# A convolution with max pooling: other steps with five products, column maxima by one reduction, another order

## The chip, the cores and the metric

The kernel runs on one core of one Trainium2 chip. The time is the device time of one execution in microseconds; where several runs were made, their median is given. The engines that matter are PE (TensorE, matrix products), DVE (VectorE), ACT (ScalarE), POOL (GpSimd) and SP (SyncE, here only for issuing transfers).

## The reference

A 3x3 convolution of 16 images, 64 input and 128 output channels, 64x64 pixels, with padding of one, and then the maximum of each 2x2 block:

```python
batch, c_in, h, w, c_out, k = 16, 64, 64, 64, 128, 3
x_pad = np.pad(x, ((0, 0), (0, 0), (1, 1), (1, 1)))
conv[b, co] += weight[co, ci, kh, kw] * x_pad[b, ci, kh:kh+h, kw:kw+w]
...
output[b, c, i, j] = np.max(conv[b, c, 2*i:2*i+2, 2*j:2*j+2])
```

Input and output are float32; the products are made of bfloat16 values and summed in float32.

## The kernel before

**Tiles.** Two images lie together on the 128 partitions, 64 input channels each. There are 8 such pairs, and each is cut into 4 quarters of 16 image rows: 32 *steps*, numbered 0 to 31 (steps 2 and 3 stand for quarters 3 and 2 of pair 0). A step yields 8 pooled rows of 64 columns, 512 numbers per output channel, for each of its two *halves* (half 0 and half 1 are the two images). 512 float32 are one bank of the accumulation memory; there are eight banks, the tiles `acc_84` to `acc_91` in the listings below. The halves' matmuls use the two row halves of the array and run side by side, as two lanes.

**Products.** For a pooled row four input rows d0 to d3 are needed. Instead of 2 x 3 tap rows on them, sums of rows and sums of weights are used. A *product* is three matmuls (the three column taps) of 512 or 504 columns for one half. There are two kinds of step.

- *Four products (W).* P2 with weights GM on d1-d2 (row sum E) and P0 with G0 on d2-d0 (part of row sum D) go into a first bank; P3 with G2 on d3-d1 (rest of D) and P1 with GP on d1+d2 (row sum S) into a second, which begins as a copy of the first after P2. That copy is the *seed* (SE, on ACT). The first bank is read out negated (EV, on ACT) to on-chip memory.
- *Five products (K).* PA1, PA2 with D2 on d2 and G0 on d0 go into the first bank, PB1, PB2 with D0 on d1 and G2 on d3 into the second, straight from the loaded rows; PR with G1 on d1+d2 (row sum KS) comes last, into the second. No seed, and one row sum in place of three.

In both kinds the maximum of the two pooled rows is taken before the last product, which is common to both rows: the row maximum (MX, on DVE, L376) puts max(second bank, EV) back in the second bank, then P1 or PR is added there. After it ACT copies the odd columns out (OD, L382), and DVE takes the maximum of the even columns in the bank and that copy (the column maximum, CM, L396) into the output tile `o` of the step, from which SP stores (ST, L416). The first bank is free after EV, the second after CM, and the next product that begins a bank takes the one that has been free longest.

**Row sums.** E, S (512 elements per partition) and D (1024) of each W step are made by POOL where `ON_GPSIMD` names them (L89, POOL), otherwise by DVE (L88, DVE); KS by DVE always. A sum on POOL waits for the last sum that DVE has before it in the order.

**Start.** Weights come in by one transfer, are cast (g0, g1, g2) and summed (D2, D0, GS, GM, GP), turned on PE against an identity (T..., L149) and copied out to `wt` (V..., L164 on ACT, L166 and L168 on DVE). Eight matmuls of ones (L524) run ahead of that. Input of pair 0 comes in seven pieces, the other pairs in two or three each (LX, issued on POOL's queue, L105), turning float32 to bfloat16 on the way. Steps 0 and 2 begin with their products cut into two half products of four pooled rows (F and H), step 1 partly (G).

**End.** The last step, 31, is worked in two parts of four pooled rows, each part's second sum in banks of its own (four banks for two halves): SL is its seeds (four copies of 256, L367), Z its P3, ML its row maxima (L372), Q its P1, ODh and CMh its odd copies and column maxima (L402, L410), U its stores (L425): before, U.0 stores part 0 of both images, U.1 and U.2 part 1 of one image each, U.1 on ACT's queue.

**Order.** The string `ORDER` lists all steps of the work by name (MX.8.1 is the row maximum of step 8, half 1), and every engine runs its own instructions in that order. A product of one half is held back until the other lane has one to go with it. Instructions wait for their data and for buffers through semaphores; an engine that waits holds all that is queued behind. Pools: 12 output tiles `o`, 14 of D, 12 each of E and S, 3 of KS, 8 each of `ev` and `od`.

## Time and profile before

| | |
|---|---|
| median of 3 runs | 101.95 us (101.53 to 102.34) |
| the profiled execution | 101.44 us, its span 99.7 us |
| granted TensorE clock, mean | 0.99 |
| matmul records | 913 |
| column maxima on DVE, step 0 to 30 | 62, mean 417 ns |
| read-outs EV on ACT | 52 negated, mean 617 ns; 12 copied, 595 ns |
| seeds on ACT | 48 of 512, mean 595 ns; 4 of 256 for the last step |
| DMA | 17.23 MB, mean 173 GB/s |

In the profile an engine's line gives its busy time, share of the span and instructions. The strips cut the span into 40 slices of 2.5 us and show the busy share of each in tenths. A group's row has the code line, engine, operation, output and input tiles with partitions x elements and type, the count, then busy time and mean ns of one, then the engine's idle time just before them with what ended it. A timeline row has the start, the length, and the instructions that ran on from one another under one line (`x2`), and in brackets an idle time before it with its releaser. Instructions of one engine overlap a little, so the distance of two starts is less than the duration of the first. Seen durations of matmuls are longer than their distance for the same reason. In the rows on transfers the last number is the time from issue to landing.

### The profile page before, as it was taken

To read this page: it belongs to the slowest core of one execution; us is meant where nothing else is said; L and a number is where in the kernel's file an instruction comes from. 1 tells how busy PE (TensorE), PEld (TensorE's weight loads), DVE (VectorE), ACT (ScalarE), POOL (GpSimd) and SP (SyncE) were. 2 spreads that over 40 slices of the span, in tenths; PEclk is the share of its full clock that TensorE was granted. 3 is DMA by queue.
4 is the path that set the end of the run, shared out by engine and by line. 5 is a ranking of instruction groups with operands and counts; after the bars stand their busy time and mean duration, and the time that the engine had idled before them with its cause. 6 is when DMAs were issued, how large, how long until landed. Compare 5 with 4: busy or idle time off the path is not lost.

```text
span 99.7 us, 2526 instructions
## 1 busy us (share of the span) xinstructions
PE 94.1 (94%) x913; PEld 60.8 (61%) x913; DVE 86.2 (86%) x192; ACT 83.2 (83%) x192; POOL 72.8 (73%) x74
## 2 busy tenths in 40 slices
PE   6999999999999999999999999999999999998830
PEld 2588864455755545566687666556578768863410
DVE  3568899999999999999999999889896899888660
ACT  5453967899898589979999988999999999999730
POOL 5996689647846992696196993994979996999300
PEclk9999999999999999999999999999999999999995
DMA  2999999999999999986709999955330285063462
GB/s 57 167 170 157 184 203 208 205 221 207 227 230 230 263 276 197 183 229 77 144 3 285 147 205 227 357 187 180 105 105 7 68 268 193 0 217 105 138 202 81
DMA packets 12316, 17.23 MB, mean 173 GB/s; under 512 B 912, under 2 KB 10256, under 8 KB 12304
## 3 DMA queue, kind: packets, MB, share of 16 engines
q0 software_dynamic: 3168, 8.39, 47.6%
q1 hardware_dynamic: 8992, 8.62, 26.6%
q8 instruction: 7, 0.11, 0.5%
q10 hardware_dynamic: 144, 0.07, 0.2%
q14 instruction: 5, 0.04, 0.1%
HBM read 17.07 MB, written 8.39 MB: 255 GB/s over the span
## 4 chain that ended last, share of the span: by engine, by line
PE 83%; ACT 9%; DVE 3%; issue 1%; DVEq 0%; ACTq 0%
PE acc L182 78%; ACT ev L342 4%; PE acc L524 4%; ACT acc L356 3%; PE acc L149 2%; ACT od L382 2%; DVE acc L376 1%; DVE acc L372 1%; DVE o L396 0%; DVE o L410 0%; ACT od L402 0%; DVEq L561 0%; DVEq L376 0%; ACTq L356 0%
## 5 line engine op out<-in xcount | busy, mean ns | idle before, releaser
L182 PEld LDWEIGHTS <-wt 64*128 64x128 bf16 x882 | 57.8, 94 | 31.5 <-issue 3.9
L182 PE MATMUL acc<-wd,wt 64*128 64x512 bf16 (+3 forms) x330 | 60.0, 365 | 0.0
L376 DVE TENSOR_TENSOR acc<-acc,ev 128x512 f32<-128x512 f32 x62 | 41.4, 694 | 3.8 <-ACT ev L342 2.0
L182 PE MATMUL acc<-ws,wt 64*128 64x512 bf16 (+3 forms) x162 | 37.4, 369 | 1.0 <-DVE acc L372 0.7
L182 PE MATMUL acc<-we,wt 64*128 64x512 bf16 (+3 forms) x162 | 36.6, 369 | 0.0
L342 ACT ACTIVATE ev<-acc 128x512 f32<-128x512 f32 x52 | 31.0, 617 | 0.6 <-PE acc L182 0.3
L356 ACT COPY acc<-acc 128x512 f32<-128x512 f32 x48 | 28.3, 595 | 3.1 <-DVE o L396 1.6
L396 DVE TENSOR_TENSOR o<-acc,od 128x256 f32<-128x256 f32 x62 | 24.5, 417 | 1.9 <-ACT od L382 1.3
L89 POOL TENSOR_TENSOR ws<-xb 128x512 bf16<-128x512 bf16 x18 | 20.6, 1155 | 6.5 <-PE acc L182 4.5
L89 POOL TENSOR_TENSOR we<-xb 128x512 bf16<-128x512 bf16 x17 | 19.5, 1154 | 7.6 <-DVE wd L88 3.9
L382 ACT COPY od<-acc 128x256 f32<-128x256 f32 x62 | 22.7, 389 | 2.2 <-PE acc L182 1.6
L89 POOL TENSOR_TENSOR wd<-xb 128x1024 bf16<-128x1024 bf16 (+1 forms) x10 | 20.3, 2030 | 5.2 <-DVE we L88 5.2
L182 PE MATMUL acc<-xb,wt 64*128 64x252 bf16 (+7 forms) x192 | 23.9, 319 | 0.0
L105 POOL DMA_DIRECT2D xb<-in_x_dram x22 | 12.2, 567 | 0.8 <-POOLq L547 0.8
L88 DVE TENSOR_TENSOR wd<-xb 128x1024 bf16<-128x1024 bf16 (+1 forms) x17 | 10.8, 667 | 0.0
L340 ACT COPY ev<-acc 128x512 f32<-128x512 f32 x12 | 6.7, 595 | 3.1 <-PE acc L182 3.1
L182 PE MATMUL acc<-ks,wt 64*128 64x504 bf16 (+1 forms) x36 | 7.3, 377 | 0.0
L524 PE MATMUL acc<-const-bfloat16-1.0 128*128 128x512 bf16 x8 | 3.6, 625 | 0.8 <-PEq L547 0.8
L88 DVE TENSOR_TENSOR we<-xb 128x512 bf16<-128x512 bf16 (+1 forms) x10 | 3.7, 391 | 0.0
L88 DVE TENSOR_TENSOR ws<-xb 128x512 bf16<-128x512 bf16 x8 | 3.3, 418 | 0.0
L88 DVE TENSOR_TENSOR ks<-xb 128x512 bf16<-128x512 bf16 x6 | 2.6, 438 | 0.7 <-DMA xb<-in_x_dram 0.7
L524 PEld LDWEIGHTS <-const-bfloat16-1.0 128*128 128x128 bf16 x8 | 1.0, 136 | 2.4 <-issue 2.4
(25 smaller groups left out, 20.2 us busy)
## 6 DMA issues: line engine op xcount, KB each, us to landing
out_dram<-o SPq DMA_DIRECT2D x31, 256.0 KB, 2.7
xb<-in_x_dram POOLq DMA_DIRECT2D x7, 496.0 KB, 10.4
xb<-in_x_dram POOLq DMA_DIRECT2D x6, 528.0 KB, 10.6
xb<-in_x_dram POOLq DMA_DIRECT2D x3, 128.0 KB, 4.5
wraw<-in_weight_dram SPq DMA_DIRECT2D x1, 288.0 KB, 2.8
xb<-in_x_dram POOLq DMA_DIRECT2D x1, 272.0 KB, 6.5
xb<-in_x_dram POOLq DMA_DIRECT2D x1, 256.0 KB, 7.2
xb<-in_x_dram POOLq DMA_DIRECT2D x1, 224.0 KB, 5.2
```

Of the source, the lines that this page charges most:

```text
L88: return on_vector(nc.vector.tensor_tensor(**args))
L89: return on_gpsimd(nc.gpsimd.tensor_tensor(**args))
L105: nc.gpsimd.dma_start(out=xb[p][:, 1 + lo : 1 + hi, :], in_=rows_of(p, lo, hi))
L149: nc.tensor.transpose(tp[:, k * CO : (k + 1) * CO], wq[:, j : j + 2, :].rearrange("a b c -> a (b c)"), ident,)
L182: nc.tensor.matmul(acc[t][:, i0:i1, o0:o1], wt[lo : lo + CI, m0 + kw - h, :], rows(lo, i0, i1, c0, c1), start=start and kw == 1, stop=True ...
L340: nc.scalar.copy(out=ev[s, h], in_=acc[t])
L342: nc.scalar.mul(ev[s, h], acc[t], -1.0)
L356: nc.scalar.copy(out=acc[tb[s, h]], in_=acc[ta[s, h]])
L376: nc.vector.tensor_tensor(out=t, in0=t, in1=ev[s, h], op=MAX)
L382: nc.scalar.copy(out=od[s, h], in_=acc[tb[s, h]][:, :, 1::2])
L396: nc.vector.tensor_tensor(out=ot[s][:, h], in0=acc[t][:, :, 0::2], in1=od[s, h], op=MAX)
L524: nc.tensor.matmul(acc[n].rearrange("p a b -> p (a b)"), ones[:, 0:128], ones, start=True, stop=True, skip_group_check=True)
```

## The change

The kinds of the steps change: five-product steps were 0, 2, 4, 10, 16 and 23, and are 0, 2, 11, 20 and 31. There are 27 four-product steps in place of 26. Since the last step is now of five products, a new function begins its second sums: `last_start` (Y) takes the two banks of a part and puts the D0 product of that part in them; Z then adds G2 on the rows themselves and Q adds G1 on KS. It has no seeds.

Sixteen column maxima (`REDUCED`) are made without ACT's odd copy: one `tensor_reduce` on DVE reads all 512 elements of the bank as pairs and writes 256 (L397 in the changed kernel).

All six turn-outs are on ACT, also that of GM and GP with the factor 0.5 (MP), and all three casts. The weight sum GS goes from POOL to DVE. The list of sums on POOL is another: of the 27 four-product steps POOL makes 17 E, 16 S and 10 D, and for step 1 the first half of E in place of the first half of D.

The order is new throughout. Among others, the loads of pairs 5 to 7 are issued one after the other, and the last step's stores end with part 0 of both halves (U.0). Line numbers shift: row maximum L384, column maximum L404, odd copy L390, read-outs L348 and L350, seed L364, half row maximum L380, odd half copy L410, column half L418, sums L87 on DVE and L88 on POOL, loads L104.

```diff
-    TYPES = "KWKWKWWWWWKWWWWWKWWWWWWKWWWWWWWW"
+    TYPES = "KWKWWWWWWWWKWWWWWWWWKWWWWWWWWWWK"
     ON_GPSIMD = """
-        Da E.3 S.3 E.5 S.5 E.6 E.7 S.9 S.6 E.13 D.11 S.8 S.11 S.13 E.17 E.14 E.15 E.18 E.12 S.12 E.19 S.17 S.18
...
+        Ea E.3 S.3 E.4 S.5 E.6 S.6 E.9 E.8 D.7 E.10 S.8 D.10 S.16 S.13 D.13 S.12 E.16 E.15 E.17 E.25 S.15 E.18
...
-    TURNED_BY_SCALAR = ("D2", "G0", "D0")
-    CAST_BY_SCALAR = ("g0", "g2")
-    REDUCED = ()
+    TURNED_BY_SCALAR = ("D2", "G0", "G2", "G1", "D0", "MP")
+    CAST_BY_SCALAR = ("g0", "g1", "g2")
+    REDUCED = ((10, 1), (13, 1), (14, 0), (14, 1), (20, 1), (18, 0), (18, 1), (21, 0), (22, 0), (23, 0), (23, 1), (24, 0), (26, 1), (27, 1), (27, 0), (30, 1))
...
     def last_product(part):
         span = (0, R // 2) if part == 0 else (R // 2, R)
-        pair_of_taps(tb, (N - 1, part), GP, step1(row["s", N - 1]), False, None, span)
+        block = GP if TYPES[N - 1] == "W" else G1
+        pair_of_taps(tb, (N - 1, part), block, step1(row["s", N - 1]), False, None, span)
+
+    def last_start(part):
+        span = (0, R // 2) if part == 0 else (R // 2, R)
+        take(tb, (N - 1, part), 0)
+        take(tb, (N - 1, part), 1)
+        pair_of_taps(tb, (N - 1, part), D0, k_rows(N - 1, 0), True, None, span)
 
     def last_edges(part):
         span = (0, R // 2) if part == 0 else (R // 2, R)
-        pair_of_taps(tb, (N - 1, part), G2, step2(row["d", N - 1], 1), False, None, span)
+        w = TYPES[N - 1] == "W"
+        rows = step2(row["d", N - 1], 1) if w else k_rows(N - 1, 2)
+        pair_of_taps(tb, (N - 1, part), G2, rows, False, None if w else R - 1, span)
...
-        "GS": lambda: sbuf_sum(False, out=gsum, in0=g0, in1=g2, op=ADD),
+        "GS": lambda: sbuf_sum("GS" not in ON_GPSIMD, out=gsum, in0=g0, in1=g2, op=ADD),
...
-        "SL": seed_last, "Z": last_edges, "ML": rowmax_half, "U": last_store,
+        "SL": seed_last, "Y": last_start, "Z": last_edges, "ML": rowmax_half, "U": last_store,
...
     ORDER = """
-        CM.2.1 CM.2.0 EV.1.0 PA1.4.1 PB1.4.1 G.2.0 MX.1.0 PA2.4.1 EV.1.1 MX.1.1 PR.0.0 LX.3.0 E.3 S.3 LX.3.1 E.5
...
+        P2.9.1 ST.2 ST.3 ST.4 ST.0 OD.6.0 CM.6.0 ST.6 ST.1 SE.9.1 PA1.11.1 P0.9.0 EV.9.0 E.8 D.7 LX.5.0 LX.5.1
+        LX.6.0 LX.6.1 LX.7.0 LX.7.1 S.10 D.12 D.14 E.13 S.7 KS.11 D.17 P2.7.1 P2.7.0 SE.7.0 P0.9.1 PA2.11.1
...
```

Three places of the order. First DVE's queue in the middle, around the column maxima of step 8; `we`, `wd`, `ws` and `ks` are the row sums E, D, S and KS. Before:

```order
L376 TENSOR_TENSOR acc_87<-acc_87,ev 128x512
L376 TENSOR_TENSOR acc_86<-acc_86,ev 128x512
L88 TENSOR_TENSOR we<-xb_102 128x512
L88 TENSOR_TENSOR ks<-xb_101 128x512
L376 TENSOR_TENSOR acc_85<-acc_85,ev 128x512
L376 TENSOR_TENSOR acc_91<-acc_91,ev 128x512
L396 TENSOR_TENSOR o<-acc_87,od 128x256
L396 TENSOR_TENSOR o<-acc_86,od 128x256
L376 TENSOR_TENSOR acc_88<-acc_88,ev 128x512
L376 TENSOR_TENSOR acc_84<-acc_84,ev 128x512
```

The rows are the row maxima of step 8, the sums E of step 20 and KS of step 16, row maxima of steps 16 and 13, the column maxima of step 8, and row maxima of step 11. After the change:

```order
L404 TENSOR_TENSOR o<-acc_84,od 128x256
L404 TENSOR_TENSOR o<-acc_86,od 128x256
L397 TENSOR_REDUCE o<-acc_90 128x256
L384 TENSOR_TENSOR acc_85<-acc_85,ev 128x512
L87 TENSOR_TENSOR we<-xb_101 128x512
L404 TENSOR_TENSOR o<-acc_87,od 128x256
L87 TENSOR_TENSOR wd<-xb_100 128x1024
L87 TENSOR_TENSOR ws<-xb_100 128x512
L384 TENSOR_TENSOR acc_84<-acc_84,ev 128x512
L404 TENSOR_TENSOR o<-acc_85,od 128x256
L384 TENSOR_TENSOR acc_89<-acc_89,ev 128x512
```

These are the column maxima of steps 8 and 11 (half 0), the reduction of step 10, the row maximum of step 8 (half 1), E of step 19, the column maximum of step 10, D of step 15 and S of step 14, the row maximum of step 12, the second column maximum of step 8, and a row maximum of step 12. Step 8's two halves now stand apart, and a reduction and three sums lie between the row maximum of its second half and the column maximum or close ahead of them.

Second, ACT's queue at the end, where `od` is an odd copy and `ev` a read-out. Before:

```order
L367 COPY acc_86<-acc_85 128x256
L367 COPY acc_90<-acc_89 128x256
L367 COPY acc_91<-acc_85 128x256
L367 COPY acc_87<-acc_89 128x256
L382 COPY od<-acc_88 128x256
L382 COPY od<-acc_84 128x256
L342 ACTIVATE ev<-acc_85 128x512
L342 ACTIVATE ev<-acc_89 128x512
L402 COPY od<-acc_87 128x128
L402 COPY od<-acc_91 128x128
L402 COPY od<-acc_86 128x128
L402 COPY od<-acc_90 128x128
```

After the change:

```order
L350 ACTIVATE ev<-acc_87 128x512
L350 ACTIVATE ev<-acc_90 128x512
L348 COPY ev<-acc_89 128x512
L348 COPY ev<-acc_91 128x512
L390 COPY od<-acc_84 128x256
L410 COPY od<-acc_85 128x128
L410 COPY od<-acc_86 128x128
L410 COPY od<-acc_90 128x128
L410 COPY od<-acc_87 128x128
```

The four seed copies are gone; the two read-outs of the last step (now copies, not negated) come ahead of one odd copy and the four half copies.

Third, POOL's queue, where the loads of pairs 5 to 7 are issued (`xb_102` to `xb_104`). Before:

```order
L89 TENSOR_TENSOR ws<-xb_98 128x512
L89 TENSOR_TENSOR we<-xb_98 128x512 x2
L89 TENSOR_TENSOR ws<-xb_99 128x512
L89 TENSOR_TENSOR ws<-xb_98 128x512
L105 DMA xb_102<-in_x_dram 128x2112
L89 TENSOR_TENSOR we<-xb_100 128x512
L89 TENSOR_TENSOR wd<-xb_99 128x1024
L89 TENSOR_TENSOR ws<-xb_99 128x512 x2
L105 DMA xb_102<-in_x_dram 128x1984
```

After the change:

```order
L88 TENSOR_TENSOR ws<-xb_98 128x512
L88 TENSOR_TENSOR we<-xb_99 128x512 x2
L88 TENSOR_TENSOR wd<-xb_98 128x1024
L104 DMA xb_102<-in_x_dram 128x2112
L104 DMA xb_102<-in_x_dram 128x1984
L104 DMA xb_103<-in_x_dram 128x2112
L104 DMA xb_103<-in_x_dram 128x1984
L104 DMA xb_104<-in_x_dram 128x2112
L104 DMA xb_104<-in_x_dram 128x1984
L88 TENSOR_TENSOR we<-xb_99 128x512
L88 TENSOR_TENSOR ws<-xb_99 128x512
L88 TENSOR_TENSOR wd<-xb_99 128x1024
```

Six loads now follow one another behind the sum D of step 7, with no sum between them.

More of the change, by code (lines that the diff above doesn't have):

```diff
@@ L520 @@
+        SE.30.0 OD.29.0 CM.29.0 OD.29.1 ST.20 ST.25 ST.19 CM.29.1 ST.28 ST.29 ST.18 D.30 P0.30.1 P3.30.1
+        PA2.31.0 P0.30.0 EV.30.1 MX.30.1 EV.30.0 P3.30.0 PA2.31.1 MX.30.0 Y.1 EV.31.0 Z.1 ML.1.0 EV.31.1 ML.1.1
+        Y.0 Z.0 ML.0.0 ML.0.1 S.30 P1.30.0 P1.30.1 OD.30.1 OD.30.0 CM.30.1 CM.30.0 ST.30 Q.1 ODh.1.0 Q.0 ODh.1.1
+        ODh.0.1 ODh.0.0 CMh.0.0 CMh.1.1 U.2 CMh.1.0 U.1 CMh.0.1 U.0
     """
```

100 lines of the change are left out of this document (47 added, 53 removed).

## The prediction

> **What bounds the kernel now.** I read the page first: the engines' busy time, the strip of 40 slices, and the chain that ended last.
>
> ```profile
> PE 94.1 (94%) x913; PEld 60.8 (61%) x913; DVE 86.2 (86%) x192; ACT 83.2 (83%) x192; POOL 72.8 (73%) x74
> ...
> PE   6999999999999999999999999999999999998830
> ...
> DVE  3568899999999999999999999889896899888660
> ...
> GB/s 57 167 170 157 184 203 208 205 221 207 227 230 230 263 276 197 183 229 77 144 3 285 147 205 227 357 187 180 105 105 7 68 268 193 0 217 105 138 202 81
> ...
> PE 83%; ACT 9%; DVE 3%; issue 1%; DVEq 0%; ACTq 0%
> ```
>
> PE is full from the fifth microsecond nearly to the end and holds 83% of the chain. DVE, though, is a strip of nines from slice 7 to 25 (15 to 62 us), with small gaps only after that. So PE bounds, and DVE stands right behind it through the middle.
>
> Next the timeline of PE, for its rate and for the end of its unbroken stretch.
>
> ```profile
> 5.77 1.47 PE L182 MATMUL acc<-xb,wt 64*128 64x256 bf16 x24
> ...
> 89.69 0.38 PE L182 MATMUL acc<-ws,wt 64*128 64x512 bf16 x1
> ...
> 89.91 0.38 PE L182 MATMUL acc<-ws,wt 64*128 64x504 bf16 x1
> ...
> 90.12 0.38 PE L182 MATMUL acc<-ws,wt 64*128 64x504 bf16 x1
> ...
> 90.99 0.38 PE L182 MATMUL acc<-ws,wt 64*128 64x512 bf16 x1
> 91.70 0.81 PE L182 MATMUL acc<-ws,wt 64*128 64x512 bf16 x5 [0.33 <-DVE acc L376]
> 92.21 1.73 PE L182 MATMUL acc<-wd,wt 64*128 64x512 bf16 x18
> ```
>
> One lane starts a matmul at 89.69, 89.91 and 90.12; the other lane's lie between, so four matmuls take 0.43: 0.1075 each. A product of one half-step (six matmuls over a pair of lanes) is 0.645, a half product 0.32. Of the 882 convolution matmuls, 36 start at 90.99 or later, so 846 lie before (by the code 714 full and 132 of half width). At that rate they need 76.8 + 7.1 us, and the last seven turns 0.4: from 5.77 that is 90.1. The row says 90.99, so PE ran at its floor for 85 us and lost 0.9. Behind it come 12 full and 24 half matmuls, 2.6 us: they could end at 93.6.
>
> DVE's own rate, from its timeline in the middle:
>
> ```profile
> 42.47 0.75 DVE L396 TENSOR_TENSOR o<-acc,od 128x256 f32<-128x256 f32 x2
> 43.13 1.29 DVE L376 TENSOR_TENSOR acc<-acc,ev 128x512 f32<-128x512 f32 x2
> 44.33 0.75 DVE L396 TENSOR_TENSOR o<-acc,od 128x256 f32<-128x256 f32 x2
> ...
> 46.40 0.68 DVE L88 TENSOR_TENSOR wd<-xb 128x1024 bf16<-128x1024 bf16 x1
> 47.00 0.42 DVE L88 TENSOR_TENSOR ks<-xb 128x512 bf16<-128x512 bf16 x1
> ...
> 48.53 0.75 DVE L88 TENSOR_TENSOR ws<-xb 128x512 bf16<-128x512 bf16 x2
> 49.20 0.69 DVE L376 TENSOR_TENSOR acc<-acc,ev 128x512 f32<-128x512 f32 x1
> ```
>
> The next start tells what one costs in a queue: row maximum 0.60, column maximum 0.33, long sum (D) 0.60, short sum (S, E, KS) 0.335.
>
> **The change, part by part.** *One product less.* 133 products in place of 134: six matmuls, -0.645, taken as **-0.6** on the path that is full. The last step's extra product in halves is within that count.
>
> *DVE's added load.* Sixteen column maxima read a whole bank instead of half. The trace has no such instruction. Its lower bound is the column maximum, 0.33, which also writes 256 elements; its upper bound is this row of POOL, 1.15:
>
> ```profile
> L382 ACT COPY od<-acc 128x256 f32<-128x256 f32 x62 | 22.7, 389 | 2.2 <-PE acc L182 1.6
> L89 POOL TENSOR_TENSOR ws<-xb 128x512 bf16<-128x512 bf16 x18 | 20.6, 1155 | 6.5 <-PE acc L182 4.5
> ```
>
> I take 0.60, the row maximum's, since that is the DVE row that reads as many elements out of the same memory. So 16 x 0.27 = +4.3 us of DVE work. Four more short sums and one KS less add 1.0, the half D 0.4. The weight turns that leave DVE return 1.8, a weight sum that comes to it costs 0.4. DVE ends with about 4 us more.
>
> The Trainium skill, "VectorE: DVE Perf Modes", section "Rules for kernel authors", speaks against this part: it says of tensor_reduce on a hot path "Expect 1× — it's the slowest DVE op", and to restructure. No row here shows the operation. By the page the cost would stand at the upper part of the bounds rather than the lower.
>
> *Whether DVE then holds PE.* For this I count DVE's lateness: the clock less its own work so far. Before, up to the middle:
>
> ```profile
> L376 DVE TENSOR_TENSOR acc<-acc,ev 128x512 f32<-128x512 f32 x26 | 17.0, 693 | 1.0 <-ACT ev L340 0.5 <-ACT od L382 0.2
> L396 DVE TENSOR_TENSOR o<-acc,od 128x256 f32<-128x256 f32 x23 | 8.7, 416 | 0.0
> L88 DVE TENSOR_TENSOR wd<-xb 128x1024 bf16<-128x1024 bf16 x10 | 6.6, 682 | 0.0
> L88 DVE TENSOR_TENSOR ks<-xb 128x512 bf16<-128x512 bf16 x5 | 2.2, 442 | 0.7 <-DMA xb<-in_x_dram 0.7
> L88 DVE TENSOR_TENSOR ws<-xb 128x512 bf16<-128x512 bf16 x4 | 1.7, 420 | 0.0
> L88 DVE TENSOR_TENSOR we<-xb 128x512 bf16<-128x512 bf16 x4 | 1.6, 418 | 0.0
> ...
> 10.48 1.30 DVE L376 TENSOR_TENSOR acc<-acc,ev 128x512 f32<-128x512 f32 x2 [0.47 <-ACT ev L340]
> ```
>
> These rows are the groups up to 44.6 us, and last DVE's first row maximum on its timeline. 26 x 0.60 + 23 x 0.335 + 10 x 0.60 + 13 x 0.335 + 0.7 for halves = 34.4; the second column maximum of the pair at 44.33 starts at 44.66, lateness 10.3. At the first row maximum it was 10.48 - 1.4 = 9.1. So it grew by 1.2 in 34 us: DVE almost never waited.
>
> In the changed order I take the column maximum of step 8, half 1, whose bank step 14's first product needs. Ahead of and with it DVE has 25 row maxima 15.0, 23 column maxima 7.7, one reduction 0.6, 11 long sums 6.6, 15 short ones 5.0, halves 0.9: 35.7 us. PE's work ahead of that product is 277 full and 132 half matmuls and seven turns: 37.3, so 43.1 from 5.77. DVE's lateness has a floor from step 2's row maximum, which needs 18 half products (5.77 + 5.8 + 0.5 = 12.1) and has 3.7 of DVE work ahead: 8.4. With the growth of before it is 9.6; I take 9.1, a little past the middle: the waits for ACT stay, but ACT has less to do. Then DVE is done at 44.8 and PE starts that product 1.8 late (1.1 to 2.3), where before lost 0.9 in all: **+0.9**. Counted along the order at these rates, a column maximum of before precedes the product that takes its bank by 4 us or more here, in the changed order by 1.7 to 2, and this stays so up to the end. So DVE becomes the bound in the middle, and the late stage has about 1.6 us to give before it costs more.
>
> *The end.* The last steps as they are:
>
> ```profile
> 91.24 1.19 ACT L367 COPY acc<-acc 128x256 f32<-128x256 f32 x4 [0.23 <-PE acc L182]
> ...
> 92.75 0.76 DVE L396 TENSOR_TENSOR o<-acc,od 128x256 f32<-128x256 f32 x2 [0.78 <-ACT od L382]
> 93.75 1.58 DVE L372 TENSOR_TENSOR acc<-acc,ev 128x256 f32<-128x256 f32 x4 [0.24 <-ACT ev L342]
> ...
> 96.21 0.49 DVE L410 TENSOR_TENSOR o<-acc,od 128x128 f32<-128x128 f32 x2 [0.17 <-ACT od L402]
> ```
>
> PE's work could end at 93.6, but the four seed copies (1.19) stand ahead of everything on ACT, DVE's half row maxima start at 93.75, and the last column maximum ends at 96.70: 3.1 behind PE's own work. With a five-product last step the seeds go; its four half row maxima are ready while PE still has step 30's and the last products. What stays behind the last matmul is one odd half copy (0.21) and up to four column halves (0.21 each, from 0.49 for two), with the reduction of step 30 (0.60) partly ahead: 1.5. So **-1.6**. Were the reduction and step 30's column maximum wholly behind, 0.6 of that goes.
>
> The final store is now of both halves:
>
> ```profile
> out_dram<-o SPq DMA_DIRECT2D x1, 128.0 KB, 1.9
> out_dram<-o SPq DMA_DIRECT2D x1, 64.0 KB, 1.7
> ...
> out_dram<-o SPq DMA_DIRECT2D x31, 256.0 KB, 2.7
> ...
> out_dram<-o SPq DMA_DIRECT2D x1, 256.0 KB, 9.8
> ```
>
> The first two rows are the last step's stores: **+0.2**.
>
> *What I cost at nothing.* Three more turn-outs and a cast go to ACT. Its rows:
>
> ```profile
> 4.14 1.70 PE L149 MATMUL acc<-ident,wq 128*128 128x128 bf16 x16
> ...
> 3.55 0.97 ACT L430 CAST wq<-wraw 128x192 bf16<-128x192 f32 x2 [1.53 <-DMA wraw<-in_weight_dram]
> 4.81 1.54 ACT L164 COPY wt<-acc 128x512 bf16<-128x512 bf16 x3 [0.29 <-PE acc L149]
> ...
> 8.19 0.62 DVE L166 TENSOR_SCALAR wt<-acc 128x896 bf16<-128x896 bf16 x1
> ```
>
> Three casts at 0.485 and the first turn-out (0.51) end at 5.5, under PE's turns, which end at 5.8; without that cover each 0.1 moves everything. The turn-out of the two middle weight sums is 0.62 as on DVE or 0.9 by ACT's 0.51 for 512 columns; at 0.9 it ends near 8.5, and the product that needs its bank comes at 8.7. ACT's relief (16 odd copies of 0.39) buys nothing: PE kept its full rate while ACT was busy. The six loads issued in one row on POOL's queue are early; behind them the stores starve, as the last row above (a store among loads, 9.8, against a median of 2.7) shows. A loads' backlog to about 47 us (an estimate: six loads of 0.5 MB at the 200 GB/s of the strip, from 32 us on) is paid by output buffers: DVE's column maximum of step 12 takes the buffer of the first store, needed at 46.6 by the count above, later ones at 49 to 62; I expect each free 2 to 4 us earlier, from loads and stores sharing that rate. Behind a column maximum that waits there, every row maximum is queued, and PE waits for those.
>
> By the Trainium skill, "DMA: Bandwidth & Descriptors", section "Queues, rings and completion order", each DMA engine takes turns between its queues packet by packet; the 9.8 against 2.7 agrees.
>
> Sum: -0.6 + 0.9 - 1.6 + 0.2 = -1.1. The profiled execution took 101.44 (span 99.7 and 1.7 around it), 0.5 under the median of 101.95. -1.1 on the median: **100.9**. With PE's lateness at its ends 100.1 to 101.3.
>
> **The rivals.** *Even:* DVE loses another 1 us, because its waits for ACT grow with a full queue on both. For it: the 1.0 of waits in the L376 row; against: ACT has 16 copies fewer. 101.95.
>
> *The reduction is dearer (slower).* The late stage holds 15 of the 16 and has 1.6 us of room: 0.11 each, so nothing happens up to 0.71. Beyond, 15 times the excess goes on the path: at 0.77 the gain is gone, at 0.84 it is 1% slower, at 0.90 +3.0 gives 103.9. For it: no row shows the operation; against: the row maximum, which reads and writes a full bank.
>
> *Buffers come late (slower).* The six loads hold back the first stores, DVE waits at step 12, and each microsecond is one of the end: two give 103.0. For it the 9.8 row, against it 2 to 4 us of room.
>
> *Better:* DVE is no later than before, 0.9, because the early stage's waits shrink: -2.0, so 99.95.
>
> **How the numbers follow.** 1% (1.02 us) is about what a measurement of this kernel can tell from no change. Forecast 0.48, of which 0.26 lies under 100.93 and 0.22 within 1%. Even 0.15 (0.10 within, 0.05 slower). Dear reduction 0.12, slower. Late buffers 0.12 (0.02 within, 0.10 slower). Better 0.13, faster. Faster 0.39, same 0.34, slower 0.27. The range goes from 99.8, just under the better case, to 103.2, over the late buffers and half of the dear reductions; about 0.15 is left out. The forecast's own range is 100.1 to 101.3.
>
> **What would show it.** First product at 5.8. The DVE strip all nines to the end, with PE's idle time put down to DVE's column maxima around step 14; PE 1 to 2 us behind its own count there. The reductions' start-to-start near 0.60; over 0.71 the dear case. No seed copies in the last step, and 1.5 between the last matmul's end and the last column maximum. DVE waits put down to DMA at its output tile mean late buffers. The forecast is wrong if the first product moves, if reductions cost more than 0.75, or if PE loses more than 3 us by 60 us.

## The result, and the profile after

The changed kernel took 102.25 us (median of 20 runs, 101.67 to 103.56), the kernel before 101.93 on the same chip (20 runs, 101.53 to 102.47): ratio 1.0038, interval 1.0021 to 1.0056. The time lies in the range given, but a gain of 1% was forecast, and the kernel became 0.4% slower.

Its first profiled execution took 103.56, the longest of all its runs. The ratios leave out single runs over 1.5% above the fastest of their kernel, such as this one. The profile after is therefore that of a further execution of the same kernel, called *again* below: 101.84 us, span 100.1, against 101.44 and 99.7 before.

Page of again: busy times, strips, shares of the chain that ended last, and the groups of DVE that changed.

```profile
PE 94.2 (94%) x913; PEld 55.5 (55%) x913; DVE 88.8 (89%) x192; ACT 83.4 (83%) x180; POOL 71.2 (71%) x72
...
PE   6999999999999999999999999999999999999910
...
DVE  3553999999999999999999999999999999895960
...
PE 83%; DMA 4%; DVE 3%; ACT 3%; issue 2%; POOL 0%; DVEq 0%; POOLq 0%
...
L384 DVE TENSOR_TENSOR acc<-acc,ev 128x512 f32<-128x512 f32 x62 | 41.0, 693 | 0.8 <-ACT ev L348 0.3
...
L397 DVE TENSOR_REDUCE o<-acc 128x256 f32<-128x512 f32 x16 | 10.9, 683 | 0.4 <-PE acc L181 0.3
L404 DVE TENSOR_TENSOR o<-acc,od 128x256 f32<-128x256 f32 x46 | 18.0, 416 | 1.2 <-DMA out_dram<-o 1.0
```

PE's strip now stays at nine two slices longer than before: the tail is repaired. DVE has nines from slice 5 to 34. Yet PE still holds 83% of the chain, and the span isn't shorter. A strip of tenths doesn't show where PE loses 2 us out of 90, so I count it: from the start of the n-th convolution matmul I take the floor of all matmuls before it (0.1075 us for a full one, half of that for half width, 0.06 for a weight turn). What is left is PE's *lateness*; it rises only where PE waits. Worked out from all matmul records, in us:

| matmul | before | again | first execution |
|---|---|---|---|
| 0 | 5.77 | 5.76 | 5.99 |
| 100 | 5.97 | 6.33 | 8.02 |
| 225 | 6.15 | 7.62 | 9.32 |
| 400 | 6.24 | 8.27 | 9.97 |
| 829 | 6.81 | 8.86 | 10.56 |
| 881, the last | 8.84 | 8.98 | 10.67 |

Before, PE lost 1.0 up to matmul 829 and then 2.0 in the tail. Now it loses 3.1 up to there and 0.1 in the tail. What the tail gives back was spent between the 100th and the 400th matmul, that is in and just behind the eight four-product steps 3 to 10 that now stand in a row, mostly by 25 us.

Those losses stand on the timeline of PE's weight loads, which carry the semaphores. Of again (the bracket is an idle time with its releaser; time in which weights could be loaded ahead is in it, so what the products lose is less):

```profile
21.25 1.19 PEld L181 LDWEIGHTS <-wt 64*128 64x128 bf16 x13 [0.44 <-DVE o L404]
...
27.64 1.19 PEld L181 LDWEIGHTS <-wt 64*128 64x128 bf16 x13 [0.27 <-DVE o L404]
...
30.32 4.43 PEld L181 LDWEIGHTS <-wt 64*128 64x128 bf16 x44 [0.31 <-ACT acc L364]
...
44.20 1.19 PEld L181 LDWEIGHTS <-wt 64*128 64x128 bf16 x13 [0.16 <-ACT acc L364]
...
71.11 5.73 PEld L181 LDWEIGHTS <-wt 64*128 64x128 bf16 x55 [0.49 <-ACT acc L364]
```

L364 is the seed copy. (A releaser is inferred: the column maxima named at 21.25 had ended by 20.86, and ACT's rows below show a seed that ended just ahead.) Put against the matmuls of the code, PE's lateness in again jumps at eleven places by 2.1 in all after the 100th matmul. Seven of them are a P0 (steps 5, 6, 6, 7, 12, 15, 23) and hold 1.35; the largest others are P2.4.0 with 0.36 and P1.1.1 with 0.19. P1.1.1 waits for a row maximum; P2.4.0, and P2.7.1 and P2.14.1 with about 0.1 each, begin 0.05 or 0.06 us after the end of the column maximum whose bank they take.

Why P0: it is added to a bank of which the seed has to be taken first, and the seed needs the end of P2. So on PE the order P2, seed on ACT, P0 is a chain through another engine. In again at P0.5.0 (half 0 of step 5), first two rows of PE's timeline, the last matmul of P2 and the first of P0, then two of ACT's, a read-out and the seed (its second):

```profile
20.07 0.38 PE L181 MATMUL acc<-we,wt 64*128 64x504 bf16 x1
...
21.25 0.37 PE L181 MATMUL acc<-wd,wt 64*128 64x512 bf16 x1
```

```profile
20.10 0.60 ACT L350 ACTIVATE ev<-acc 128x512 f32<-128x512 f32 x1
20.62 0.58 ACT L364 COPY acc<-acc 128x512 f32<-128x512 f32 x1
```

P2's last matmul ends at 20.45, the seed runs from 20.62 to 21.20, P0 starts at 21.25: 1.18 us from start to start. On this lane the order has one product between, so PE itself is ready after 0.215 + 0.645 = 0.86. The wait is the difference, 0.32. With two products between, PE would be ready at 1.5, and nothing would be seen. Counted in the order: before, such a pair with one product between stands at P0.6.1 and in the last step (P0.31.0, P0.31.1). In the changed order there are eight: P0.3.0, 5.0, 6.1, 6.0, 7.0, 12.0, 15.0 and 23.0. The seven P0 at which PE waits are seven of these eight; that of step 3 is hidden behind P1.1.1's wait. At all seven the seed begins 0.03 to 0.18 us after P2's last matmul ends, and P0 0.05 or 0.06 after the seed.

### The profile page after: what moved, and what is told of

It is laid out like the page before. It is cut to its first block, busy times and chain, and to the rows that moved or that the text cites. A ratio compares the mean times of both kernels' runs of the same rounds, so it can differ in the third digit from the quotient of the medians.

```text
span 101.8 us, 2518 instructions
## 1 busy us (share of the span) xinstructions
PE 94.9 (93%) x913; PEld 56.0 (55%) x913; DVE 88.6 (87%) x192; ACT 83.4 (82%) x180; POOL 71.3 (70%) x72
## 4 chain that ended last, share of the span: by engine, by line
PE 79%; DMA 7%; DVE 3%; ACT 3%; POOL 2%; issue 2%; DVEq 0%; POOLq 0%
PE acc L181 79%; DMA xb<-in_x_dram 7%; POOL xb L104 1%; DVE wd L87 1%; DVE o L404 1%; ACT acc L364 1%; DVE o L418 1%; ACT od L390 1%; ACT od L410 1%; DVE acc L384 0%; ACT ev L350 0%; POOL ident masks.py:199 0%; POOL ident masks.py:197 0%; DVEq L569 0%; POOLq L555 0%
## 5 line engine op out<-in xcount | busy, mean ns | idle before, releaser
L181 PEld LDWEIGHTS <-wt 64*128 64x128 bf16 x882 | 53.0, 94 | 37.5 <-issue 5.7
L181 PE MATMUL acc<-wd,wt 64*128 64x512 bf16 (+2 forms) x336 | 62.6, 369 | 0.2
L384 DVE TENSOR_TENSOR acc<-acc,ev 128x512 f32<-128x512 f32 x62 | 41.0, 693 | 0.6 <-ACT ev L350 0.2
L181 PE MATMUL acc<-ws,wt 64*128 64x512 bf16 (+1 forms) x162 | 37.1, 377 | 0.0
L350 ACT ACTIVATE ev<-acc 128x512 f32<-128x512 f32 x54 | 31.9, 602 | 2.2 <-PE acc L181 1.1
L364 ACT COPY acc<-acc 128x512 f32<-128x512 f32 x52 | 29.6, 582 | 2.7 <-DVE o L404 1.0
L88 POOL TENSOR_TENSOR we<-xb 128x512 bf16<-128x512 bf16 (+1 forms) x18 | 20.1, 1126 | 9.1 <-DMA xb<-in_x_dram 5.1
L88 POOL TENSOR_TENSOR ws<-xb 128x512 bf16<-128x512 bf16 x16 | 18.4, 1153 | 9.9 <-DVE wd L87 3.7
L88 POOL TENSOR_TENSOR wd<-xb 128x1024 bf16<-128x1024 bf16 x10 | 21.2, 2128 | 1.9 <-DVE ws L87 0.9
L181 PE MATMUL acc<-xb,wt 64*128 64x256 bf16 (+6 forms) x180 | 20.7, 306 | 1.1 <-DMA xb<-in_x_dram 1.1
L404 DVE TENSOR_TENSOR o<-acc,od 128x256 f32<-128x256 f32 x46 | 18.0, 417 | 1.2 <-DMA out_dram<-o 1.0
L390 ACT COPY od<-acc 128x256 f32<-128x256 f32 x46 | 16.6, 377 | 2.8 <-PE acc L181 2.5
L104 POOL DMA_DIRECT2D xb<-in_x_dram x22 | 12.0, 568 | 0.8 <-POOLq L555 0.8
L87 DVE TENSOR_TENSOR wd<-xb 128x1024 bf16<-128x1024 bf16 (+1 forms) x18 | 11.4, 655 | 0.0
L397 DVE TENSOR_REDUCE o<-acc 128x256 f32<-128x512 f32 x16 | 10.9, 682 | 0.4 <-PE acc L181 0.3
L348 ACT COPY ev<-acc 128x512 f32<-128x512 f32 x10 | 5.6, 586 | 3.8 <-PE acc L181 3.8
L87 DVE TENSOR_TENSOR ks<-xb 128x512 bf16<-128x512 bf16 x5 | 2.1, 421 | 4.8 <-DMA xb<-in_x_dram 4.8
L181 PE MATMUL acc<-ks,wt 64*128 64x504 bf16 (+3 forms) x36 | 5.8, 341 | 0.0
L87 DVE TENSOR_TENSOR ws<-xb 128x512 bf16<-128x512 bf16 x11 | 4.4, 418 | 0.0
L87 DVE TENSOR_TENSOR we<-xb 128x512 bf16<-128x512 bf16 (+1 forms) x10 | 3.9, 403 | 0.0
```

Source lines behind the costliest of these rows:

```text
L87: return on_vector(nc.vector.tensor_tensor(**args))
L88: return on_gpsimd(nc.gpsimd.tensor_tensor(**args))
L104: nc.gpsimd.dma_start(out=xb[p][:, 1 + lo : 1 + hi, :], in_=rows_of(p, lo, hi))
L181: nc.tensor.matmul(acc[t][:, i0:i1, o0:o1], wt[lo : lo + CI, m0 + kw - h, :], rows(lo, i0, i1, c0, c1), start=start and kw == 1, stop=True ...
L348: nc.scalar.copy(out=ev[s, h], in_=acc[t])
L350: nc.scalar.mul(ev[s, h], acc[t], -1.0)
```

## The experiments

Each was measured beside the kernel before on the same chip (101.80 to 101.99 us). Lateness is counted as above.

**The start.** The same kernel again, and again with the load of the first input piece ahead of the identity:

```diff
-La Lb g0 ID D2 TD2 A1 A2 B1 B2 C ...
+La Lb A1 g0 ID D2 TD2 A2 B1 B2 C ...
```

> The changed kernel as it is, for a profile of a usual execution. Theory of the start (the first input pieces land later than DVE's queue and PE need them, and DVE's lateness from there is kept to the end): the median stays near 102.2; in the profile PE is late already by 20 us (start of a matmul less the work before it: over 8 where the kernel before has 6), and from 30 us on loses at most 1 us more. Theory of the middle (DVE's heavier load does it): PE starts like the kernel before, late by 6, and loses 3 or more between 25 and 90 us.

> Only the third input piece is issued on POOL ahead of the identity, as in the kernel before. Theory of the start: the pieces A1 and A2 land about 0.5 us earlier, the second row sum KS on DVE starts so much earlier, and the time falls by 0.3 to 0.6 us. Theory of the middle: no change, within 0.15 us.

Again: 102.08 (12 runs, 101.68 to 103.01), ratio 1.0032 (1.0009 to 1.0054). a1_first: 101.92, 1.0017 (0.9992 to 1.0041). Neither theory holds alone: again is 6.33 late at matmul 100, near the 5.97 of before, and loses 2.65 after it, 1.29 of that by matmul 225. DVE's row sum KS of step 2 needs the fourth piece; on DVE's timeline of the first execution, and then of again:

```profile
11.14 0.42 DVE L87 TENSOR_TENSOR ks<-xb 128x512 bf16<-128x512 bf16 x1 [4.21 <-DMA xb<-in_x_dram]
```

```profile
8.82 0.43 DVE L87 TENSOR_TENSOR ks<-xb 128x512 bf16<-128x512 bf16 x1 [1.92 <-DMA xb<-in_x_dram]
```

The piece came 2.3 later in the first execution, PE was 1.7 later at matmul 100 (8.02 against 6.33) and still 1.7 at the last (10.67 against 8.98), and the time was 1.72 longer. What PE loses there it never makes up. In these two executions and in the profiled ones of seven variants below (a1_first, ks2_late, sums_left_out, copies_left_out, d4_left_out, both_left_out, swap_one) the span less the lateness at matmul 100 is 93.75 to 93.78 us, so they differ only by what happened before that matmul. That it was the landing of the input each time isn't shown. The load's place changes little: PE is 6.40 late at matmul 100 in a1_first, and the loss after it is the same 2.65.

**One sum moved behind a row maximum.** KS.2 behind MX.0.0 on DVE:

```diff
-... GS GP GM KS.0 KS.2 g1 TG1 ... MX.0.1 EV.0.0 MX.0.0 H.0.0
+... GS GP GM KS.0 g1 TG1 ... MX.0.1 EV.0.0 MX.0.0 KS.2 H.0.0
```

> Only the row sum KS of step 2, which waits for the fourth input piece, is moved behind the two row maxima of step 0 on DVE. Theory of the start, in its form that DVE's wait for that piece is what is carried: the first row maximum starts 1 us or more earlier than the landing, and the time falls by 0.5 to 1.2 us. If the same landing holds PE itself (step 2's products read the piece), the time falls by less than 0.3 us. Theory of the middle: no change.

102.77, ratio 1.0095 (1.0072 to 1.0118). POOL's sum for step 1 waits for the last sum that DVE has before it, and PE waits for that; POOL's and PE's timeline of ks2_late:

```profile
11.20 0.67 POOL L88 TENSOR_TENSOR we<-xb 128x256 bf16<-128x256 bf16 x1 [4.45 <-DVE ks L87]
```

```profile
11.92 0.83 PE L181 MATMUL acc<-we,wt 64*128 64x256 bf16 x12 [0.90 <-POOL we L88]
```

0.9 later at matmul 100, 0.9 later at the last, and 0.95 in the time of the two profiled executions (102.79 against 101.84; 0.7 by the medians). A wait on PE in the first 12 us costs its full length.

**Without the reductions.** All 16 as before, by odd copy and maximum:

```diff
-    REDUCED = ((10, 1), (13, 1), (14, 0), ...)
+    REDUCED = ()
```

> All column maxima by ACT's odd copy and DVE's maximum of two, as in the kernel before: DVE loses 16 x 0.27 = 4.3 us of work, ACT gets 16 copies more (4.3 us at 0.27 from start to start). Theory of the middle: DVE is no longer the bound, the time falls by 1 us or more. Theory of the start: PE's lateness at 25 us stays, what it loses after that shrinks; the time changes by -0.6 to +0.6, since ACT, with its copies back, takes DVE's place.

109.19, ratio 1.0722 (1.0693 to 1.0751): 7 us slower. DVE has 16 x 0.27 = 4.3 less to do, but the waits of no_reduce (total, times, longest) read:

```profile
ACT od L390 <- PE acc L181: 8.1, 15, 1.4
DVE o L404 <- ACT od L390: 6.5, 9, 1.6
```

In the new order the 16 copies stand in ACT's queue close behind the product that they need. ACT waits at its head, and DVE behind ACT. This prices the old copies only for places that weren't made for them. A second try moved each copy to just ahead of its column maximum:

```diff
-... P0.12.0 P3.12.1 OD.10.1 CM.10.1 ...
+... MX.10.0 OD.10.1 CM.8.0 ... P0.12.0 P3.12.1 CM.10.1 ...
```

> The changed kernel with ACT copies and maxima of two in place of the 16 reductions, as in the run without reductions, but each copy stands in ACT's queue just ahead of its column maximum (two DVE instructions before it, never before its last product), not directly behind the last product. If the 7 us of that run came from ACT waiting at its head for products: most of it goes, 102 to 104. If they came from ACT's load of 4.3 us: 106 or more.

111.32, from one run at a granted clock of 1.0. Here four of the copies come ahead of products that are held back for the other lane, so that these odd columns lack their last product. The expected 102 to 104 didn't come; waits at ACT's head remain (9.0 us for PE in its profile, taken at a granted clock of 0.968). What the reductions are worth against copies in an order built for them stays open.

**More work on DVE, in both kernels.** Row sums made twice, D of steps 5 and 6 (+1.2 us of DVE) or S of steps 14, 19 and 24 (+1.0):

```diff
+        for _ in range(2 if s in (5, 6) else 1):
             sbuf_sum(f"D.{s}" not in ON_GPSIMD, ...)
```

> The kernel before, with the same two row sums made twice (at 17 and 20 us): 1.2 us of DVE work more. If PE bounds it and DVE has room behind it, as the prediction counted (4 us in the middle): less than 0.4 more than 101.9. If DVE bounds this kernel too: 1.0 to 1.3 more.

> The changed kernel, with the row sums D of steps 5 and 6 on DVE (at 17 and 21 us) made twice: 2 x 0.60 = 1.2 us of DVE work more, nothing else. If DVE bounds the changed kernel from there to the end: the time grows by 1.0 to 1.3 over the 102.1 of the unchanged one, so 103.1 to 103.4. If DVE has the 1.7 to 2 us of room that the prediction counted: by less than 0.4.

> The kernel before, with the row sums S of steps 14, 19 and 24 (at about 38, 52 and 61 us) made twice: 1.0 us of DVE work. If DVE has room in the kernel before: less than 0.3 more than 101.9. If not: 0.8 to 1.1 more.

> The changed kernel, with the row sums S of steps 14, 19 and 24 on DVE (at about 44, 57 and 79 us) made twice: 3 x 0.335 = 1.0 us of DVE work. If DVE bounds to the end: 0.8 to 1.1 more than 102.1, so 102.9 to 103.2. If the late stage has the 1.6 us of room of the prediction: less than 0.3 more.

| | time | ratio | last matmul's lateness |
|---|---|---|---|
| early_before | 103.11 | 1.0115 (1.0093 to 1.0137) | 10.39 (before 8.84) |
| early_after | 103.45 | 1.0150 (1.0121 to 1.0179) | 10.51 (again 8.98) |
| late_before | 103.21 | 1.0113 (1.0089 to 1.0138) | 10.20 |
| late_after | 103.58 | 1.0155 (1.0129 to 1.0181) | 10.47 |

Against its own kernel (ratio 1, or 1.0038 for the changed one) each costs 1.1 to 1.2 us, about what was added, in the old kernel as in the new. So the 4 us by which a column maximum precedes the product that takes its bank are no room: before the bank is wanted, a row maximum is wanted by the last product, and a row sum by the next. The weight loads of late_before show one such place, a D sum that PE stood waiting for:

```profile
36.34 13.92 PEld L182 LDWEIGHTS <-wt 64*128 64x128 bf16 x132 [0.67 <-DVE wd L88]
```

In before the same row stands at 35.86, with 0.30 in place of 0.67.

**Less work on DVE.** Three row sums left out (S of step 4, E of step 5 and D of step 6 are replaced by sums of the steps 1, 4 and 5), 1.2 us; and in another kernel the 16 reductions replaced by a copy of the even columns, so that the odd ones don't count:

```diff
-            nc.vector.tensor_reduce(out=ot[s][:, h], in_=acc[t].rearrange(...), axis=..., op=MAX)
+            nc.vector.tensor_copy(out=ot[s][:, h], in_=acc[t][:, :, 0::2])
```

> The changed kernel without three row sums that DVE makes at 19 to 23 us: S of step 4, E of step 5 and D of step 6 are left out, and the sums of steps 1, 4 and 5 are used in their place, so the outputs of steps 4, 5 and 6 are other numbers. DVE loses 0.335 + 0.335 + 0.60 = 1.27 us of work there. If the row sums that stand ahead of row maxima early on are what makes PE late (1.25 us between matmuls 150 and 225 in the trace of the unchanged kernel): PE's lateness at matmul 225 falls by 0.9 to 1.2 and the time by as much, to 100.9 to 101.2. If the ring of PE, ACT and DVE sets it whatever the sums: less than 0.3.

> The changed kernel with the 16 reductions replaced by a copy of the even columns on DVE (256 elements read, not 512): the odd columns are left out of those maxima. DVE loses 16 x 0.27 = 4.3 us, 15 of the 16 behind 47 us; ACT stays as it is. If DVE's load bounds the late stage: what PE loses behind matmul 400 (0.7 us in the trace) goes, and the last reduction's 0.27 in the tail: 101.1 to 101.4. If the reductions are hidden in the room of the late stage: 101.9 to 102.2.

sums_left_out: 102.21, 1.0036 (1.0010 to 1.0063). even_only: 102.00, 1.0021 (0.9995 to 1.0047). The group row of even_only on DVE:

```profile
L397 DVE COPY o<-acc 128x256 f32<-128x256 f32 x16 | 6.7, 417 | 0.9 <-PE acc L181 0.9
```

417 ns in place of 683, so DVE had 4.2 us less, and PE gained nothing: the loss after matmul 100 is 2.64 and 2.63, against 2.65. DVE now waits for PE instead. Only the tail of even_only is 0.2 shorter (span less lateness at matmul 100: 93.57). But 15 of its 16 reductions lie behind 47 us, where little is lost; for the middle it is sums_left_out that counts: DVE waited 0.43 at CM.3.1, and P0.5.0 still began 0.31 late.

**Less work on ACT, and one more sum off DVE.** Odd copies of steps 1 and 3 left out, their column maxima copy the even columns (1.1 us of ACT); D of step 4 replaced by that of step 3; and both:

```diff
+            elif s in (1, 3):
+                nc.vector.tensor_copy(out=ot[s][:, h], in_=acc[t][:, :, 0::2])
...
+            if s == 4:
+                row["d", s] = row["d", 3]
+                return
```

> The changed kernel without ACT's four odd copies of steps 1 and 3 (17 to 22 us): DVE copies the even columns there in the same time, the odd columns of these steps are left out. ACT loses 4 x 0.27 = 1.1 us. If ACT's full queue makes the products P0 of steps 5 and 6 wait for their seeds (0.32, 0.13 and 0.29 us at 21 to 25 us in the trace of the unchanged kernel): these three waits go, the wait of P2 of step 4 (0.36) stays, and the time falls by 0.5 to 0.8, to 101.3 to 101.6. If the seeds wait for banks that DVE frees: no change.

> The changed kernel without the row sum D of step 4 (DVE, 16.9 us; the sum of step 3 is used in its place). It stands ahead of the column maxima whose bank the first product P2 of step 4 takes. If DVE sets that wait: the 0.36 us at P2 of step 4 go, the waits of P0 of steps 5 and 6 stay, the time falls by 0.3 to 0.4. If ACT sets all of them: no change.

> Both of the two together: if the waits lie one after the other, on ACT and on DVE, the gains add up to 0.8 to 1.2, so 100.9 to 101.3. If the one wait is replaced by the other, not more than the larger of the two.

101.98 (1.0013, 0.9983 to 1.0043), 102.18 (1.0017, 0.9989 to 1.0044), 102.36 (1.0048, 1.0013 to 1.0083). The loss after matmul 100 is 2.67, 2.64 and 2.67. Without D.4 the wait of 0.36 at P2.4.0 is gone, so DVE's queue did set that one. But P1.3.0 then waits 0.37: it needs a row maximum that needs P3.3.0, with one product between, the same kind of loop through DVE (in d4_left_out P3.3.0 ends at 18.05, the row maximum runs from 18.16 to 18.86, P1.3.0 starts at 18.91). With both relieved, P0.5.0 still waits 0.31, although ACT then stands idle for 0.15 ahead of its seed.

**The distance itself.** In the changed kernel, P3.4.0 ahead of P0.5.0, which gives P0.5.0 one product more of distance; in the kernel before, which has no such pair there, three planted: P0.13.1, P0.12.1 and P0.24.0 each ahead of the P1 that stood before them. No work is added in either.

```diff
-CM.3.1 P0.5.0 P3.4.0 MX.4.0
+CM.3.1 P3.4.0 P0.5.0 MX.4.0
```

```diff
-P2.14.0 P1.11.1 SE.13.1 P0.13.1
+P2.14.0 SE.13.1 P0.13.1 P1.11.1
```

> The changed kernel with two products of PE's order exchanged: P3 of step 4 (half 0) goes ahead of P0 of step 5 (half 0), so that two products and not one lie between P2 of step 5 and its P0. If the distance sets the wait: the 0.32 us at that product go, the other waits stay; the time falls by 0.1 to 0.35, less where a row maximum that had been hidden behind it comes next. If engine load sets it: the wait of 0.3 stays at the same place in time, on the exchanged product or on the next.

> The kernel before with three pairs of products of PE's order exchanged: P0 of step 13 (half 1), of step 12 (half 1) and of step 24 (half 0) each go ahead of the product P1 that stood before them, so that one product and not two lies between P2 and P0. ACT, DVE and POOL keep their work and their order. If the distance sets the waits: 0.2 to 0.4 us of PE wait at each of the three, none of it made up later, and the time grows by 0.6 to 1.1, to 102.5 to 103.0. If load sets them: within 0.2 of 101.9.

planted: 104.42, ratio 1.0251 (1.0216 to 1.0285). PE's weight loads in planted:

```profile
44.83 2.92 PEld L182 LDWEIGHTS <-wt 64*128 64x128 bf16 x29 [0.42 <-issue]
...
50.42 2.92 PEld L182 LDWEIGHTS <-wt 64*128 64x128 bf16 x29 [0.82 <-issue]
...
73.04 1.82 PEld L182 LDWEIGHTS <-wt 64*128 64x128 bf16 x18 [0.61 <-issue]
```

These are P0.13.1, P0.12.1 and P0.24.0. By the matmuls PE loses 0.26, 0.70 and 0.49 there and another 1.0 at four products that follow; the time is 2.5 longer, where 0.6 to 1.1 was expected. ("issue" is a wait with no releaser in the records; here the code and the place name it.) A pair brought near costs what the chain through ACT needs, with what ACT's queue holds ahead of the seed, and the cost stays to the end: at P0.13.1 the seed began 0.14 after P2's end, at P0.12.1 0.79 after it, behind another seed and a read-out. The exchange also makes three P1 one product later, and with them the maxima behind; which of the two causes the four later waits isn't separated.

swap_one: 102.10, ratio 1.0023 (1.0002 to 1.0044). P0.5.0's 0.32 is gone, but P0.6.1 waits 0.20 in place of 0.13 and P0.6.0 0.52 in place of 0.29:

```profile
25.32 2.47 PEld L181 LDWEIGHTS <-wt 64*128 64x128 bf16 x24 [0.64 <-issue]
```

The loss after matmul 100 is again 2.65. One pair mended alone gives nothing, and the traces show what took its place. The seed of step 5, half 1, takes the bank that the column maximum CM.3.1 frees; DVE's and then ACT's timeline of swap_one:

```profile
23.08 0.42 DVE L404 TENSOR_TENSOR o<-acc,od 128x256 f32<-128x256 f32 x1
```

```profile
23.58 0.57 ACT L364 COPY acc<-acc 128x512 f32<-128x512 f32 x1
```

ACT was free from 23.45, but the column maximum ended at 23.50, at the end of a DVE queue without a gap since 13.25. Behind this seed ACT has a read-out and the seed of P0.6.0. In again the same column maximum ended at 23.07 and the seed began at 23.15, without a pause on ACT. So two chains held PE level here: the near pair through ACT, and DVE's queue. sums_left_out relieved the second, swap_one the first, and no run relieved both.

The Trainium skill, "Perfetto Trace Analysis", section "Optimization Strategy", advises to find the gaps on the bound engine and make what they wait for come sooner or finish faster. That found the waits here, but at one gap at a time (swap_one, d4_left_out) it only moved them.

**The tail alone.** The kernel before with its last step as the changed kernel has it (five products, `last_start`, no seeds), and the rest of its order as it was:

```diff
-    TYPES = "KWKWKWWWWWKWWWWWKWWWWWWKWWWWWWWW"
+    TYPES = "KWKWKWWWWWKWWWWWKWWWWWWKWWWWWWWK"
...
+PA1.31.1 PA1.31.0 PA2.31.1 PA2.31.0 EV.31.0 Y.1 Z.1 ML.1.0 EV.31.1 ML.1.1 P1.30.0 P1.30.1 Y.0 Z.0 ML.0.0 ML.0.1
```

> The kernel before with one part of the change alone: step 31 is of five products, with the four-bank start and the changed kernel's order of the last step; the kinds of all other steps, the order, the turn-outs and the column maxima stay as they were. One product more (+0.65 on PE), no seed copies for the last step, three row sums less on POOL, one more on DVE. If the tail is worth what the two profiles show (PE loses 2.0 us behind matmul 829 before, nothing after; 0.6 more behind PE's end, 0.3 more for the last store): 0.65 - 2.0 + 0.6 + 0.3 = -0.45, 101.4. If the tail is worth nothing by itself: 102.5.

102.63, ratio 1.0092 (1.0062 to 1.0122). PE's losses in the tail shrink from 2.0 to 0.6 (7.26 late at matmul 829, 7.87 at the last, 8.84 before), and its last matmul ends 0.3 earlier, although PE was 0.3 later than in before at matmul 100. But step 30's two column maxima are late, and two large stores stand ahead of the last ones; DVE's and SP's timelines:

```profile
94.95 0.75 DVE L404 TENSOR_TENSOR o<-acc,od 128x256 f32<-128x256 f32 x2
```

```profile
87.35 9.26 SPq L424 DMA_DIRECT2D out_dram<-o  x6
96.70 1.17 SPq L433 DMA_DIRECT2D out_dram<-o  x2
```

The large stores (L424) are issued until 96.6, before until 94.4. The last store landed at 99.57, before at 98.47. In again step 30's column maxima end no earlier than here (95.77 against 95.70), but only one large store comes behind them, and the last store lands 2.1 after DVE's last column maximum rather than 3.0. So a tail without seeds is worth something only with the stores out of its way.

**A version meant to be better.** In the changed kernel reductions also for (1, 1) and (3, 0), and five sums moved later (D.5, D.8, D.9, S.9, D.17):

```diff
-    REDUCED = ((10, 1), ...
+    REDUCED = ((1, 1), (3, 0), (10, 1), ...
-P1.1.1 D.5 D.4 OD.2.1 ... CM.1.0 P3.3.1
+P1.1.1 D.4 OD.2.1 ... CM.1.0 D.5 P3.3.1
```

> Nothing is left out. Two more column maxima (step 1 half 1, step 3 half 0) are reductions, which takes 0.54 us off ACT ahead of the seeds of step 5; the sum D of step 5 stands behind the column maximum of step 1 and not ahead of it; S of step 9, D of step 8 and D of step 17 are made later, where they are still early enough. If early ACT and the column maxima are the cause: the waits at P2 of step 4 (0.36) and at P0 of steps 5 and 6 (0.74) shrink by 0.6 or more together, and the time falls to 101.2 to 101.6, under the kernel before. If DVE's added 0.54 us is passed on to PE: 102.1 to 102.6.

104.22, ratio 1.0231 (1.0186 to 1.0277). It waits 0.71 at P0.5.0, 0.50 at P1.3.0 and 0.78 in all at step 11's PR. No version beat both kernels; a1_first, at 101.92, is level with before.

## Why the prediction failed

The spans are 99.7 and 100.1, +0.4. By the forecast's own terms:

| term | forecast | measured |
|---|---|---|
| one product less | -0.6 | -0.65 |
| PE's lateness before the tail | +0.9 | +2.2 |
| the end | -1.6 | -1.45 |
| the last store | +0.2 | +0.3 |
| sum | -1.1 | +0.4 |

The second row is the last matmul's lateness in again less that of matmul 829 before, 8.98 - 6.81: 0.36 by the 100th matmul, 1.81 after it. The third is the 2.03 that PE lost in the tail before, less 0.58 that now lie behind its last start (1.66 to the last column maximum's end, 1.08 before).

**The step that failed: +0.9 for PE's lateness.** The forecast worked it out at one place, the product of step 14 that takes the bank of the column maximum of step 8, half 1: DVE done there at 44.8, the product 1.8 late, and nothing more lost behind it. The two rows in again, of DVE's and of PE's timeline:

```profile
45.18 0.41 DVE L404 TENSOR_TENSOR o<-acc,od 128x256 f32<-128x256 f32 x1
```

```profile
45.64 0.37 PE L181 MATMUL acc<-we,wt 64*128 64x512 bf16 x1
```

The column maximum ends at 45.59 and the product follows at 45.64, so this hand-over is indeed tight. But the product is 2.6 late (8.35 by the count, less 5.76), 0.8 more than taken, because DVE was later from its start:

```profile
9.52 1.30 DVE L384 TENSOR_TENSOR acc<-acc,ev 128x512 f32<-128x512 f32 x2 [0.28 <-ACT ev L348]
10.98 0.29 DVE L87 TENSOR_TENSOR we<-xb 128x256 bf16<-128x256 bf16 x1 [0.16 <-DMA xb<-in_x_dram]
...
12.82 1.30 DVE L384 TENSOR_TENSOR acc<-acc,ev 128x512 f32<-128x512 f32 x2
```

The last row is step 2's row maxima. The forecast put them at 12.1, counting PE's products alone; DVE came to them at 12.82, after these waits and the 1.92 for the fourth piece. And from step 14's product to its last matmul PE lost another 0.6 (8.35 to 8.98), where the forecast saw a stage with 1.6 to give. With the 0.1 that before lost more than the 0.9 taken, 0.8 + 0.6 - 0.1 is the 1.3 between forecast and measurement.

What the forecast never looked at is the chain P2, seed, P0 through ACT, which holds 1.35 us of the waits in again; it saw that PE kept its rate while ACT was busy, and concluded that ACT's place in the order cost nothing. That held only because the order of before kept two products or more between such a pair everywhere but at P0.6.1 and in the last step. That the chain makes PE wait is shown by the seven places, by planted, and by swap_one, where the one wait went. That these pairs by themselves set the total of 2.65 isn't shown: where swap_one took one away, DVE's queue held PE just as long.

**Room of 1.6 us and of 4 us: false.** It was counted at the bank. The doubled sums show none, in either kernel.

**DVE as the bound in the middle: half right.** In again DVE had 29.9 us of work, at the forecast's rates, between the row maximum at 14.79 and the column maximum at 45.18, and took 30.4 for it. It ran at its own floor and has no slack to lose (1.1 to 1.2 for about as much work added). But it doesn't bound alone: with 1.27 us of its sums left out, PE lost as much as in again. Work and order meet at the same limit, and relief of one engine alone leaves the other hand-overs as they are. At the column maximum of step 8, half 1, DVE's lateness was 9.9 (45.59 - 35.7) where 9.1 was taken; its floor was 9.1 (12.82 - 3.7) rather than 8.4.

**The reductions: right.** One starts 0.60 before the next instruction in the queue, as taken. DVE's timeline of again in the tail:

```profile
94.76 0.68 DVE L397 TENSOR_REDUCE o<-acc 128x256 f32<-128x512 f32 x1
95.36 0.41 DVE L404 TENSOR_TENSOR o<-acc,od 128x256 f32<-128x256 f32 x1
95.89 0.89 DVE L418 TENSOR_TENSOR o<-acc,od 128x128 f32<-128x128 f32 x4
```

The Trainium skill, "VectorE: DVE Perf Modes", section "Rules for kernel authors", warns that tensor_reduce is the slowest operation of that engine; here it costs as much as the row maximum that reads as many elements of the bank (683 and 693 ns), and the dear rival falls.

**The end: right.** The four half column maxima end at 96.78; PE's last matmul ended at 95.39, from this row of PE's timeline:

```profile
94.45 0.94 PE L181 MATMUL acc<-ks,wt 64*128 64x256 bf16 x12
```

1.4 behind it, forecast 1.5. From there to the end of the span are 3.3, before 3.0.

**Late buffers: didn't come.** The loads landed by about 52 us rather than 47, yet DVE waits for a store only once, 1.0 us at 91 us (the L404 row of the page), when PE's rows show no wait for it.

**Even, the rival nearest in time, came by another way.** It wanted DVE's waits for ACT to grow. They shrank; the waits of before, then of again:

```profile
DVE acc L376 <- ACT ev L342: 2.0, 7, 0.5
...
DVE o L396 <- ACT od L382: 1.3, 3, 0.8
```

```profile
DVE acc L384 <- ACT ev L348: 0.3, 1, 0.3
...
DVE o L404 <- ACT od L390: 0.2, 1, 0.2
```

**First product at 5.8: right** in again (5.76) and nearly in the first execution (5.99). But the 100th matmul came 0.36 later than before in again and 2.05 in the first execution, by pieces of the input that land after the first; the forecast didn't price them.

## What to carry to other kernels

When one engine runs at its floor, every wait on it is kept to the end, so count its lateness against its own work, instruction by instruction; a strip of nines hides 2 us. In an order written by hand, look at each chain that leaves the full engine and comes back (product, copy on another engine, next product on the copy), and count how much of the engine's own work lies between: if it is less than the chain takes, it waits, however free the other engine is. The room before one hand-over is worth nothing while a nearer one has none. Two chains can stand level, and then mending a single wait, or relieving a single engine, leaves the total where it was.

## What the runs showed of the hardware

The time from issue to landing of the first loads varies from run to run: the fourth input piece, of one and the same program, was there at 11.05 us in the first execution and at 8.73 in again; that is 1.7 us of the time.

From the last matmul's start on a bank over a copy of that bank on ACT to the first matmul on the copy it took 1.18 us at P0.5.0: 0.38 of matmul, 0.17 until the copy starts, 0.58 of copy, 0.05 until the matmul starts.

The loss after matmul 100 is the same within 0.04 us (2.63 to 2.67) in the changed kernel's two executions and eight variants of it whose load on DVE or ACT, start or local order differed. At one place the traces show two chains that hold it, the near pair and DVE's queue; how much would go if both were relieved, and by which order, stays open.
